# Half of the attention transposes of six head pairs moved from TensorE to VectorE squares and a trip through DRAM

## The chip, the cores and the metric

The kernel runs on one core of a Trainium2 chip: TensorE (PE, its weight loads PEld), VectorE (DVE), ScalarE (ACT), GpSimd (POOL) and SyncE (SP), which only issues transfers. The metric is the time of one execution on the device in microseconds.

## What is computed

One layer with batch 1, 1024 positions and width 1024, in float32. The normalised input is modulated and projected to queries, keys, values and gates of 16 heads of width 64. Eight heads are stick-breaking, eight are forgetting attention. Each is causal, in blocks of 128 queries:

```python
# forgetting head, query block qs:ke
s = q[qs:ke] @ k[:ke].T * scale + (f_q[:, None] - f_k[None, :])
p = softmax(where(k_pos <= q_pos, s, -inf));  out = p @ v[:ke]
# stick-breaking head
z = q[qs:ke] @ k[:ke].T * scale
log_keep = where(k_pos < q_pos, log_sigmoid(-z), 0)
later = cumsum(log_keep, reverse=True) - log_keep
w = where(k_pos < q_pos, exp(log_sigmoid(z) + later), 0);  out = w @ v[:ke]
```

The outputs are gated, go through one output projection, and a residual with a second normalisation ends the layer.

## The kernel before

Heads are worked in pairs p = 0 to 7; pairs 0 to 3 are stick-breaking, 4 to 7 forgetting. Float32 products are made from two rounded parts: an operand is split into a high part (a cast) and a low part (a subtraction), and two or three matmuls are added up. A **unit** (p, h, i) is head h of pair p with query block i; it has i+1 key blocks of 128 columns. Within a head units run with i rising in pairs 0 to 3 and falling in pairs 4 to 6.

The main loop goes over the 128 units with step k. In step k TensorE gets, in this order: the scores of unit k (`att_scores`, L427 and L428), some matmuls of the projections of later pairs (`fill`: lines L270 to L272 for queries, keys and gates, L327 to L329 for values), a product with the values if one is ready (`att_pv`, L493), the transposes of unit k-2 (`att_transpose`, L478; LAG is 2), and more `fill`. A product takes two neighbouring units, so that of the first of the two comes four steps after its scores. TensorE's order is fixed by the program; those of the other engines and of SyncE are made by a scheduler when the program is built, and each runs its queue strictly in order.

In pairs 0 to 3 the scores S go through two sigmoids on ScalarE (L447, L448), a scan on VectorE (L453, L457) and a product with GpSimd (L461). The scan's second operand is a constant kept in PSUM. In pairs 4 to 7 VectorE adds the forget rows `fb` and takes the row's extreme (L434), ScalarE makes the exponential and its sum (L440), VectorE the reciprocal (L441), GpSimd the scaled rows (L442). Then TensorE turns each 128x128 block into PSUM tile T (L478), ScalarE casts T to the high part (L480) and VectorE subtracts for the low part (L481). After the product, ScalarE, VectorE and GpSimd make the gated output `ty` (L512 to L514), and SyncE writes it to DRAM (L522). VectorE adds the causal mask to `fb` ahead of time (L412), from a PSUM copy except the first time.

GpSimd also splits all projection weights (`fetch_w`, L123 to L126; SyncE loads them by L121), and beside pairs 3 to 5 the output projection's, scaled by the gate, which SyncE writes to DRAM (L830, L831) and nobody reads before pair 7.

Tiles that matter: S has one buffer of two banks; T two; the pool `att`, from which `kp`, `be`, `a` and `fb` come, six of 128x1024.

Of the kernel before, what the change touches and what calls it, by code (L numbers as in the profile page):

```python
# [13 lines left out]
P = 128  # L14
# [13 lines left out]
def tile_hybrid_layer(  # L28
# [82 lines left out]
    f_dr = dr.tile([8, SEQ], F32, tag="f_dr", name="f_dr")  # L111

# [132 lines left out]
    def evac_k(p, ch, acc, kst, klo, heads):  # L245
        s = slice(ch * 512, ch * 512 + 512)
        for h in heads:
            r = slice(h * HD, h * HD + HD)
            o = slice((1 - h) * HD, (1 - h) * HD + HD)
            first = nc.scalar.copy(kst[h][r, s], acc[r, :])  # L250
            kf = kst[h].bitcast(F32)
            nc.sync.dma_start(kf[o, s], kf[r, s])
            if p not in CASTS_FIRST:
                last = nc.vector.tensor_tensor(klo[r, s], acc[r, :], kf[r, s], op=ALU.subtract)
        if p in CASTS_FIRST:
            for h in heads:
                r = slice(h * HD, h * HD + HD)
                last = nc.vector.tensor_tensor(klo[r, s], acc[r, :], kst[h].bitcast(F32)[r, s], op=ALU.subtract)  # L258
        return first, last
# [106 lines left out]
    def forget_rows(lf):  # L366
# [17 lines left out]
        nc.sync.dma_start(f_dr.rearrange("h (t p) -> (h t) p", p=P), fr)  # L384
# [22 lines left out]
    def att_causal(u):  # L407
        p, h, i = u
        if p >= 4:
            f = fb[2 * (p - 4) + h]  # L410
            dg = slice(i * P, i * P + P)
            nc.vector.tensor_tensor(f[:, dg], f[:, dg], ps_causal[0][:, :P] if ps_causal else causal, op=ALU.add)  # L412

    def att_scores(u, following):
# [4 lines left out]
        w = ke // ns  # L419
        qs = slice(i * P, i * P + P)  # L420
# [3 lines left out]
        S = s_tile(f"S_{p}_{h}_{i}")  # L424
        for s in range(ns):
            ks = slice(s * w, s * w + w)
            nc.tensor.matmul(S[:, s, :w], qst[p][h][:, qs], kst[p][h][:, ks], start=True, stop=False)  # L427
            nc.tensor.matmul(S[:, s, :w], z, klo[p][:, ks], start=False, stop=True)  # L428
        v3 = lambda a: a[:, :ke].rearrange("p (a b) -> p a b", a=ns)
        if p >= 4:  # L430
# [3 lines left out]
            rows = nc.vector.tensor_tensor_reduce(out=v3(a), in0=S[:, :ns, :w], in1=v3(f),  # L434
# [7 lines left out]
            nc.gpsimd.tensor_scalar(a[:, :ke], a[:, :ke], l, 1.0, op0=ALU.mult, op1=ALU.mult)  # L442
            st_w[u] = a
        else:
# [17 lines left out]
            nc.gpsimd.memset(be[:, ke - 1:ke], 0.0)  # L462
            st_w[u] = be

    def att_transpose(u):
        p, h, i = u
        a = st_w.pop(u)
        j, qo = i // 2, (i % 2) * P
        for g in range((i // 4) + 1):
            n = min(4, i + 1 - 4 * g)  # L470
            if (p, h, j, g) not in st_pt:
                st_pt[p, h, j, g] = [pt_tile(x, f"pt{x}_{p}_{h}_{j}_{g}", F32R, [P, 4, 256])
                                     for x in range(2)]
            hi, lo = st_pt[p, h, j, g]
            tp = t_tile(f"T_{p}_{h}_{i}_{g}")
            for b in range(n):
                kb = 4 * g + b
                nc.tensor.transpose(tp[:, b * P:(b + 1) * P], a[:, kb * P:(kb + 1) * P], ident)  # L478
            t3 = tp[:, :n * P].rearrange("p (a b) -> p a b", a=n)
            nc.scalar.copy(hi[:, :n, qo:qo + P], t3)  # L480
            nc.vector.tensor_tensor(lo[:, :n, qo:qo + P], t3, hi.bitcast(F32)[:, :n, qo:qo + P],  # L481
                                    op=ALU.subtract)
# [521 lines left out]
    for k in range(len(units) + LAG + 1):  # L1004
        if k < len(units):
# [13 lines left out]
            if 4 <= p < NPAIR - 1 and i == 0:  # L1019
                load_fb(2 * (p - 4) + h + 2)  # L1020
# [3 lines left out]
        if LAG <= k < len(units) + LAG:  # L1024
            u = units[k - LAG]
            att_transpose(u)
            seen.add(u)
            if (u[0], u[1], u[2] ^ 1) in seen:
# [76 lines left out]
```

## Time and profile before

| what | value |
|---|---|
| time, median of 3 runs | 685.13 us (685.02 to 685.16) |
| the profiled execution's own time | 685.25 us |
| its span | 683.5 us |
| TensorE clock granted | 0.999 |
| start of the first scores of pair 1, 4, 5, 6, 7 | 137.64, 346.13, 419.02, 489.29, 551.66 us |
| DMA moved | 81.60 MB, 45036 packets |

In the rows of the profile a group reads: line, engine, operation, output<-input by the program's names, shapes, count, then busy time and mean duration in ns, then idle time of the engine just ahead and who ended it. A row of the timeline begins with start and duration in us. A row of DMA issues ends with size and median time from issue to landing. A row of stretches gives for each engine the busy time in that stretch, then clock, DMA share and GB/s. Matmuls overlap, so their durations add up to more than the time that they take.

### The profile page before, as it was taken

Reading aid. Unit: us, or ns where it says so; the run is one execution under the profiler, and the core shown is the slowest. Engines: PE = TensorE matmul, PEld = TensorE weight load, DVE = VectorE, ACT = ScalarE, POOL = GpSimd, SP = SyncE. Lnnn points to the kernel's source line nnn. Section 1 sums busy time; section 2 is a strip of 40 time slices with the busy share of each in tenths; the row PEclk is TensorE's granted clock in tenths of the full one; section 3 lists DMA queues with packets and bytes.
Section 4 is the critical chain, followed back from the end, with each engine's and each line's share of the span. In section 5 each row is a group of like instructions: output and inputs, shape, how many; then the busy total and the mean of one; then the engine's idle time right before and its main releaser. Section 6 shows DMA issues by size and latency. Waiting matters only on the chain.

```text
span 683.5 us, 11770 instructions
## 1 busy us (share of the span) xinstructions
PE 667.2 (98%) x4021; PEld 587.2 (86%) x4021; DVE 450.6 (66%) x914; ACT 382.0 (56%) x861; POOL 427.7 (63%) x558
## 2 busy tenths in 40 slices
PE   5999999999999999999999999999999999999995
PEld 4789898888998888889988888899988889888885
DVE  6785368867666667676675665765566677774645
ACT  5668357856567666566675564655565667531000
POOL 5558977756348566556388896877584364665411
PEclk9999999999999999999999999999999999999999
DMA  9966231112102121122144563453341298143301
GB/s 338 410 236 233 82 105 44 41 29 60 29 9 86 27 57 54 37 55 55 55 131 136 172 176 121 143 166 129 101 150 40 72 327 318 58 162 118 123 31 62
DMA packets 45036, 81.60 MB, mean 119 GB/s; under 512 B 5232, under 2 KB 18864, under 8 KB 44976
## 3 DMA queue, kind: packets, MB, share of 16 engines
q1 hardware_dynamic: 43536, 76.63, 33.8%
q10 hardware_dynamic: 1440, 4.21, 2.2%
q8 instruction: 32, 0.52, 0.3%
q14 instruction: 28, 0.23, 0.1%
HBM read 60.34 MB, written 16.29 MB: 112 GB/s over the span
## 4 chain that ended last, share of the span: by engine, by line
PE 94%; DMA 3%; DVE 2%; ACT 0%; issue 0%; POOL 0%; DVEq 0%
PE m L270 10%; PE m L272 10%; PE m L271 10%; PE pv L493 10%; PE T L478 9%; PE S L428 5%; PE S L427 5%; PE o L884 4%; PE o L882 4%; PE o L883 4%; PE v L327 4%; PE v L328 4%; PE v L329 4%; DMA raws<-in_w_qkg_dram 2%; PE st_late L589 1%; PE st_q L589 1%
## 5 line engine op out<-in xcount | busy, mean ns | idle before, releaser
L270 PE MATMUL m<-uh,whi 128*128 128x512 f32 x304 | 126.4, 416 | 0.0
L272 PE MATMUL m<-uh,wlo 128*128 128x512 f32 x304 | 119.7, 394 | 0.0
L271 PE MATMUL m<-ul,whi 128*128 128x512 f32 x304 | 119.7, 394 | 0.0
L481 DVE TENSOR_TENSOR pt<-T,pt 128x512 fp32r<-128x512 f32 (+2 forms) x192 | 100.5, 550 | 17.5 <-ACT pt L480 16.5
L461 POOL TENSOR_TENSOR be<-be,kp 128x127 f32<-128x127 f32 (+3 forms) x64 | 77.2, 1207 | 33.1 <-DVE kp L457 23.5
L480 ACT CAST pt<-T 128x512 fp32r<-128x512 f32 (+2 forms) x192 | 85.8, 480 | 16.1 <-PE T L478 12.5
L453 DVE TENSOR_TENSOR_SCAN kp<-kp,floor 128x512 f32<-128x512 f32 (+2 forms) x64 | 65.2, 1018 | 31.2 <-ACT kp L447 30.1
L493 PEld LDWEIGHTS pv<-pt,v 128*128 128x128 f32 (+1 forms) x640 | 77.1, 163 | 4.4 <-DVE pt L481 0.7
L493 PE MATMUL pv<-pt,v 128*128 128x256 f32 (+3 forms) x640 | 80.4, 271 | 0.5 <-DVE pt L481 0.5
L442 POOL TENSOR_SCALAR a<-a,l 128x1024 f32<-128x1024 f32 (+3 forms) x64 | 48.1, 751 | 40.3 <-DVE l L441 26.7
L272 PEld LDWEIGHTS m<-uh,wlo 128*128 128x128 f32 x304 | 57.1, 188 | 13.6
L440 ACT ACTIVATE a<-a,nm 128x1024 f32<-128x1024 f32 (+3 forms) x64 | 49.8, 778 | 33.8 <-DVE nm L434 32.7
L427 PE MATMUL S<-k,q 128*128 128x512 f32 (+5 forms) x192 | 66.5, 348 | 0.2 <-DVE nm L434 0.2
L428 PE MATMUL S<-kl,qz 128*128 128x512 f32 (+5 forms) x192 | 65.5, 342 | 0.0
L270 PEld LDWEIGHTS m<-uh,whi 128*128 128x128 f32 x304 | 57.3, 188 | 8.5 <-DVE kl L258 0.2
L271 PEld LDWEIGHTS m<-ul,whi 128*128 128x128 f32 x304 | 57.4, 189 | 8.0
L434 DVE CUSTOM_DVE_ANT_0 a<-S,fb 128x1024 f32<-128x1024 f32 (+3 forms) x64 | 48.3, 755 | 20.1 <-PE S L428 9.3
L514 POOL TENSOR_TENSOR ty<-ty,sg 64x256 f32<-64x256 f32 x64 | 47.5, 742 | 22.3 <-DVE ty L513 11.1
L447 ACT ACTIVATE kp<-S 128x128 f32<-128x128 f32 (+3 forms) x64 | 41.7, 652 | 31.6 <-PE S L428 29.4
L327 PE MATMUL v<-whi_v,uh 128*128 128x256 f32 (+1 forms) x192 | 56.0, 292 | 0.0
L405 ACT CAST qz<-q 64x128 fp32r<-64x128 f32 x128 | 37.4, 295 | 33.2 <-PE S L428 31.8
L328 PE MATMUL v<-whi_v,ul 128*128 128x256 f32 (+1 forms) x192 | 54.2, 282 | 0.0
(285 smaller groups left out, 1593.6 us busy)
## 6 DMA issues: line engine op xcount, KB each, us to landing
raw<-in_w_qkg_dram SPq DMA_DIRECT2D x38, 256.0 KB, 2.9
wss<-in_w_ss_dram SPq DMA_DIRECT2D x16, 512.0 KB, 8.4
x<-in_x_dram SPq DMA_DIRECT2D x8, 512.0 KB, 6.9
k<-k SPq DMA_DIRECT2D x32, 128.0 KB, 2.3
wg<-in_w_gate_dram SPq DMA_DIRECT2D x8, 512.0 KB, 4.9
raw_o<-in_w_out_dram SPq DMA_DIRECT2D x16, 256.0 KB, 2.8
fb<-f_dr ACTq DMA_DIRECT2D x8, 512.0 KB, 4.3
wo_dr<-whi_o SPq DMA_DIRECT2D x16, 256.0 KB, 2.5
```

Source lines behind the costliest of these rows:

```text
L270: nc.tensor.matmul(acc, hi[:, c], u_hi[kt][:, s], start=(kt == 0), stop=False)
L271: nc.tensor.matmul(acc, hi[:, c], u_lo[kt][:, s], start=False, stop=False)
L272: nc.tensor.matmul(acc, lo[:, c], u_hi[kt][:, s], start=False, stop=(kt == NB - 1))
L327: nc.tensor.matmul(acc[:, :n], u_hi[kt][:, ts_], hi[:, s], start=(kt == 0), stop=False)
L328: nc.tensor.matmul(acc[:, :n], u_lo[kt][:, ts_], hi[:, s], start=False, stop=False)
L427: nc.tensor.matmul(S[:, s, :w], qst[p][h][:, qs], kst[p][h][:, ks], start=True, stop=False)
L428: nc.tensor.matmul(S[:, s, :w], z, klo[p][:, ks], start=False, stop=True)
L453: scan = nc.vector.tensor_tensor_scan(rv, rv, floor[0][:, 512 - n:][:, ::-1], initial=0.0, op0=ALU.mult, op1=ALU.max)
L461: nc.gpsimd.tensor_tensor(be[:, :ke - 1], be[:, :ke - 1], kp[:, 1:ke], op=ALU.mult)
L480: nc.scalar.copy(hi[:, :n, qo:qo + P], t3)
L481: nc.vector.tensor_tensor(lo[:, :n, qo:qo + P], t3, hi.bitcast(F32)[:, :n, qo:qo + P], op=ALU.subtract)
L493: nc.tensor.matmul(acc[:m, q0:256], vt[p][:, kb, h * P:h * P + m], pt[:, kb % 4, q0:], start=start, stop=stop)
```

## The change

In pairs 1 to 6 one unit of every two neighbours, the one that comes first in the head's order (i even in pairs 1 to 3, odd in 4 to 6), is no longer turned by TensorE. VectorE transposes each 32x32 square of its rows (into the finished `kp` tile in pairs 1 to 3, into a new `att` tile `sq` in 4 to 6), SyncE writes the result to a DRAM tile `far`, and after that four transfers read it back, one for each 32 target partitions, in runs of (i+1) x 128 bytes. The rows come back turned, in SBUF. ScalarE casts them as it did T; the low part is subtracted by GpSimd in pairs 4 to 6 and for the second group of four key blocks in pairs 1 to 3, by VectorE for the first group there. In pairs 4 to 6 the scaling of a moved unit's rows goes from GpSimd to ScalarE. A moved unit's cast and subtraction are issued together with its neighbour's transposes, one step later than its own transposes were. The forget rows of the next head are loaded one step later. `quartered` is false for every pair, so what depends on it stays as it was; the cut below leaves it out.

```diff
+    def by_blocks(t, n, natural):
+        return t[:, :n * P].rearrange("p (k s c) -> p k s c" if natural else "p (s k c) -> p k s c", k=n, s=4)
+    def on_dma(u):
+        p, h, i = u
+        return i % 2 == (p >= 4) and 0 < p < NPAIR - 1
...
-            nc.gpsimd.tensor_scalar(a[:, :ke], a[:, :ke], l, 1.0, op0=ALU.mult, op1=ALU.mult)
+            if moved:
+                nc.scalar.activation(a[:, :ke], a[:, :ke], AF.Copy, scale=l)
+                squares = att_tile(f"sq_{p}_{h}_{i}")
+                nc.vector.transpose(by_blocks(squares, i + 1, False), by_blocks(a, i + 1, True))
+                through_dram(u, squares, a)
+            else:
+                nc.gpsimd.tensor_scalar(a[:, :ke], a[:, :ke], l, 1.0, op0=ALU.mult, op1=ALU.mult)
...
             nc.gpsimd.memset(be[:, ke - 1:ke], 0.0)
+            if moved:
+                nc.vector.transpose(by_blocks(kp, i + 1, False), by_blocks(be, i + 1, True))
+                through_dram(u, kp, be)
...
+    def through_dram(u, src, dst):
+        p, h, i = u
+        ke, run = (i + 1) * P, (i + 1) * 32
+        far = dr.tile([P, SEQ], F32, tag="far", bufs=4, name=f"far_{p}_{h}_{i}")
+        nc.sync.dma_start(far[:, :ke], src[:, :ke])
+        for s in range(4):
+            nc.sync.dma_start(dst[s * 32:s * 32 + 32, :ke].rearrange("k (q r) -> k q r", q=4),
+                              far[:, s * run:s * run + run].rearrange("(q k) r -> k q r", q=4))
...
+            if on_dma(u):
+                full = a[:, :(i + 1) * P].rearrange("p (q k c) -> p k q c", q=4, c=32)[:, 4 * g:4 * g + n]
+                parts = [t[:, :n, qo:qo + P].rearrange("p k (q c) -> p k q c", q=4)
+                         for t in (hi, hi.bitcast(F32), lo)]
+                nc.scalar.copy(parts[0], full)
+                eng = nc.gpsimd if p >= 4 or g else nc.vector
+                eng.tensor_tensor(parts[2], full, parts[1], op=ALU.subtract)
+                continue
...
-            if 4 <= p < NPAIR - 1 and i == 0:
-                load_fb(2 * (p - 4) + h + 2)
+            if k > 64 and i == NB - 1 and units[k - 1][2] == 0 and 2 * (p - 4) + h + 1 < 8:
+                load_fb(2 * (p - 4) + h + 1)
...
-            att_transpose(u)
+            other = (u[0], u[1], u[2] ^ 1)
+            if not on_dma(u):
+                att_transpose(u)
+                if on_dma(other):
+                    att_transpose(other)
```

On VectorE, in pair 2, head 0, the rows between the scan of unit 6 (`kp_2_0_6`) and that of unit 7 read before:

```order
L457 SCALAR_TENSOR_TENSOR kp_2_0_6_2806<-kp_2_0_6_2806,floor_882 128x384
L513 TENSOR_TENSOR ty_2_0_1_2830<-pv_2_0_1_2821,ty_2_0_1_2830 64x256
L481 TENSOR_TENSOR pt1_2_0_2_0_2836<-T_2_0_4_0_2837,pt0_2_0_2_0_2835 128x4x128
L481 TENSOR_TENSOR pt1_2_0_2_1_2845<-T_2_0_4_1_2846,pt0_2_0_2_1_2844 128x128
L242 SCALAR_TENSOR_TENSOR q_3_0_2686<-m_3_0_1_2781,q_3_0_2686 64x512
L453 SCALAR_TENSOR_TENSOR kp_2_0_7_2865<-kp_2_0_7_2865,floor_882 128x512
```

The same place now (`pt1` is a low part, `T` a turned block in PSUM, `be` the weights of a unit in SBUF):

```order
L513 SCALAR_TENSOR_TENSOR kp_2_0_6_2833<-kp_2_0_6_2833,floor_882 128x384
L550 TENSOR_TENSOR pt1_2_0_2_0_2916<-be_2_0_4_2736,pt0_2_0_2_0_2915 128x4x128
L593 TENSOR_TENSOR ty_2_0_1_2864<-pv_2_0_1_2855,ty_2_0_1_2864 64x256
L255 SCALAR_TENSOR_TENSOR q_3_0_2706<-m_3_0_1_2804,q_3_0_2706 64x512
L520 STREAM_TRANSPOSE kp_2_0_6_2833<-be_2_0_6_2834 128x7x4x32
L509 SCALAR_TENSOR_TENSOR kp_2_0_7_2884<-kp_2_0_7_2884,floor_882 128x512
```

The subtraction of unit 4 takes both inputs from SBUF, and comes first; the squares of unit 6 are new and stand behind it and two others.

On SyncE, from the end of pair 4 into pair 5, the queue read before:

```order
L522 DMA y_dr_91<-ty_4_1_1_5131 64x256
L121 DMA raw_v3_2_5529<-in_w_v_dram 128x512
L121 DMA raw_v3_3_5535<-in_w_v_dram 128x512
L522 DMA y_dr_91<-ty_4_1_0_5224 64x256
L121 DMA raw_o5_1_5570<-in_w_out_dram 128x512
```

The same place now (`far` is the DRAM tile of a moved unit, `wo_dr` the output projection's split weights in DRAM):

```order
L529 DMA far_5_0_7_5163<-sq_5_0_7_5161 128x1024
L602 DMA y_dr_91<-ty_4_1_1_5190 64x256
L910 DMA wo_dr_92<-whi_o4_1_5359 128x512
L911 DMA wo_dr_92<-wlo_o4_1_5360 128x512
L134 DMA raw_v3_0_5572<-in_w_v_dram 128x512
L531 DMA a_5_0_7_5153<-far_5_0_7_5163 32x4x256 x4
L910 DMA wo_dr_92<-whi_o5_0_5502 128x512
L529 DMA far_5_0_5_5263<-sq_5_0_5_5261 128x768
```

Between the write of a unit's squares and its four reads stand an output's write, two writes of split weights and a load.

More of the change, by code (lines that the diff above doesn't have):

```diff
@@ L246, in evac_k, with made, home @@
         s = slice(ch * 512, ch * 512 + 512)
+        def made(t, r):
+            return t[r, :].rearrange("p (k s c) -> p k s c", k=4, s=4) if quartered(p) else t[r, :]
+        def home(t, r):
+            if not quartered(p):
+                return t[r, s]
+            return t[r, :].rearrange("p (s k c) -> p k s c", s=4, c=32)[:, 4 * ch:4 * ch + 4]
         for h in heads:
@@ L383, in forget_rows @@
         nc.scalar.copy(fr, ft)
-        nc.sync.dma_start(f_dr.rearrange("h (t p) -> (h t) p", p=P), fr)
+        if quartered(4):
+            for hh in range(8):
+                nc.sync.dma_start(f_dr[hh].rearrange("(s t c) -> t s c", s=4, c=32),
+                                  fr[8 * hh:8 * hh + 8, :].rearrange("t (s c) -> t s c", s=4))
+        else:
+            nc.sync.dma_start(f_dr.rearrange("h (t p) -> (h t) p", p=P), fr)
         yield
@@ L411, in att_causal @@
             dg = slice(i * P, i * P + P)
[L412 removed]
+            tri = ps_causal[0][:, :P] if ps_causal else causal
+            fd = f[:, dg]
+            if quartered(p):
+                fd = f.rearrange("p (s k c) -> p k s c", s=4, c=32)[:, i]
+                tri = tri.rearrange("p (s c) -> p s c", s=4)
+            nc.vector.tensor_tensor(fd, fd, tri, op=ALU.add)
     def att_scores(u, following):
@@ L419, in att_scores @@
         w = ke // ns
+        moved = on_dma(u)
+        quarters = quartered(p)
+        run = (i + 1) * 32
         qs = slice(i * P, i * P + P)
```

38 lines of the change are left out of this document (29 added, 9 removed).

## The prediction

> **What bounds the kernel now.** I read the page first (which engine is full, at which clock), then the chain that ended last by line, then the busy time of each engine by stage, with the stages cut where the first scores of pairs 1, 4, 5, 6 and 7 start, then groups by shape for the prices.
>
> ```profile
> span 683.5 us, 11770 instructions
> PE 667.2 (98%) x4021; PEld 587.2 (86%) x4021; DVE 450.6 (66%) x914; ACT 382.0 (56%) x861; POOL 427.7 (63%) x558
> ...
> by line: PE m L270 10.3%; PE m L272 10.2%; PE m L271 10.2%; PE pv L493 10.0%; PE T L478 9.1%; PE S L428 4.9%; PE S L427 4.9%; PE o L884 4.4%; PE o L882 4.4%; PE o L883 4.4%; PE v L327 4.2%; PE v L328 4.1%; PE v L329 4.1%; DMA raws<-in_w_qkg
> ```
>
> ```profile
> core 0: us, PE busy (x) PEld busy (x) DVE busy (x) ACT busy (x) POOL busy (x), PEclk, DMA share, GB/s
> 137.64:346.13 208.49, 208.49 (x1363) 189.28 (x1361) 142.17 (x237) 134.66 (x303) 120.78 (x167) 1.00 0.17 48
> 346.13:419.02 72.89, 72.89 (x423) 63.42 (x422) 45.22 (x114) 41.09 (x98) 62.66 (x69) 1.00 0.50 155
> 419.02:489.29 70.27, 70.27 (x491) 65.13 (x490) 44.08 (x119) 39.78 (x104) 50.94 (x58) 1.00 0.38 120
> 489.29:551.66 62.37, 62.11 (x360) 53.30 (x358) 41.76 (x109) 38.50 (x93) 35.86 (x44) 1.00 0.38 110
> ```
>
> The first window holds pairs 1 to 3, the others pairs 4, 5 and 6: all that the change touches. TensorE is busy in 413.76 of these 414.02 us, at clock 1.00, and the chain runs almost wholly over its lines. So in this stretch whatever leaves TensorE shortens the kernel, as long as nothing else makes TensorE wait. The second thing to see is GpSimd in pair 4: 62.66 of 72.89 us, far above VectorE and ScalarE.
>
> **What leaves TensorE.** In pairs 1 to 3 the moved units are i = 0, 2, 4, 6 with 1+3+5+7 = 16 of a head's 36 blocks, in pairs 4 to 6 i = 1, 3, 5, 7 with 20. Six heads each: 96 + 120 = 216 of the 576 transposes. The price of one is not its busy time, since matmuls overlap, but its share of the chain: 9.1% of 683.5 us over 576 is 0.108 us. The timeline agrees:
>
> ```profile
> 241.62 0.39 PE L272 MATMUL m<-uh,wlo 128*128 128x512 f32 x1
> 241.85 0.82 PE L478 MATMUL T<-ident,be 128*128 128x128 f32 x6
> 242.43 0.48 PE L270 MATMUL m<-uh,whi 128*128 128x512 f32 x1
> 242.74 0.39 PE L271 MATMUL m<-ul,whi 128*128 128x512 f32 x1
> ```
>
> From 241.85 to 242.74 stand six transposes and one product; a product takes 0.23 (241.62 to 241.85), which leaves 0.66, or 0.11 each. 216 x 0.108 = 23.3 us: 10.4 in pairs 1 to 3, 8.6 in 4 and 5, 4.3 in 6. No matmul is added or made longer. [...]
>
> **What is added to engines beside TensorE.** The prices:
>
> ```profile
> L481 DVE TENSOR_TENSOR pt<-T,pt 128x512 fp32r<-128x512 f32 x96 | 64.6, 686 | 16.8 <-ACT pt L480 16.3
> L481 DVE TENSOR_TENSOR pt<-T,pt 128x128 fp32r<-128x128 f32 x32 | 9.0, 281 | 0.1
> L480 ACT CAST pt<-T 128x512 fp32r<-128x512 f32 x96 | 54.8, 587 | 7.7 <-PE T L478 5.0
> L447 ACT ACTIVATE kp<-S 128x1024 f32<-128x1024 f32 x8 | 8.2, 1028 | 3.5 <-PE S L428 3.5
> L442 POOL TENSOR_SCALAR a<-a,l 128x1024 f32<-128x1024 f32 x8 | 9.0, 1130 | 5.1 <-DVE l L441 5.1
> L442 POOL TENSOR_SCALAR a<-a,l 128x256 f32<-128x256 f32 x8 | 3.9, 487 | 6.1 <-DVE l L441 3.2 <-PE v L329 2.8
> L126 POOL TENSOR_TENSOR wlo<-raw,whi 128x512 fp32r<-128x512 f32 x38 | 49.1, 1297 | 2.4 <-DMA wo_dr<-wlo_o 0.8
> L453 DVE TENSOR_TENSOR_SCAN kp<-kp,floor 128x512 f32<-128x512 f32 x40 | 48.8, 1219 | 24.3 <-ACT kp L447 23.7 <-issue 0.2
> ```
>
> The trace shows no transpose by squares. From below it is the subtraction's slope, (686 - 281)/384 = 1.05 ns a column, so 1.2 us for 1024; from above the scan's 1219/512 = 2.4 ns, so 2.4 us. I take 1.2, since one pass over one input is the nearer kind. VectorE then gets 16 x 128 columns, about 2.7 us, in a head of pairs 1 to 3, and hands 0.8 us of subtractions to GpSimd; in pairs 4 to 6 it gets 3.3 and hands over 3.5. ScalarE scales rows instead of GpSimd (at most 1.03 us for 1024 columns); its casts only change their source. At 68% and 65% in pairs 1 to 3 and less later, both have room: nothing on the sum.
>
> GpSimd has not. In pairs 4 to 6 it loses four scalings a head, between 1.13 and 0.49, 3.2 us, and gains the subtraction of 2560 columns at 1.297/512, 6.5 us: plus 3.3 a head, 6.6 a pair. Pair 4: 62.7 + 6.6 = 69.3 us of work in 72.9 - 4.3 = 68.6; pair 5: 57.5 in 66.0. It just fits if the output projection's splits, which nobody awaits here, run a little earlier; it leaves no slack.
>
> **The new path, and who waits at its end.** A product of two units comes four units after the first one's scores, before and after. Two heads show the room:
>
> ```profile
> 235.18 0.37 PE L428 MATMUL S<-kl,qz 128*128 128x448 f32 x1
> ...
> 254.62 1.64 PE L493 MATMUL pv<-pt,v 128*128 128x256 f32 x13
> ...
> 384.93 0.39 PE L428 MATMUL S<-kl,qz 128*128 128x512 f32 x1
> ...
> 403.44 1.73 PE L493 MATMUL pv<-pt,v 128*128 128x256 f32 x14
> ```
>
> In pair 2 the last score of unit 6 ends at 235.55 and its product starts at 254.62: 19.1 us, less 12 blocks no longer turned in between, 17.8. In pair 4, unit 7: 385.32 to 403.44, 18.1 less 10 blocks, 17.0. What must fit there:
>
> ```profile
> L434 DVE CUSTOM_DVE_ANT_0 a<-S,fb 128x1024 f32<-128x1024 f32 x8 | 9.7, 1216 | 2.1 <-PE S L428 2.1
> L440 ACT ACTIVATE a<-a,nm 128x1024 f32<-128x1024 f32 x8 | 9.2, 1152 | 6.4 <-DVE nm L434 6.4
> L440 ACT ACTIVATION_READ_ACCUMULATOR a<-a,nm 128x1 f32 x64 | 12.0, 187 | 0.0
> L441 DVE RECIPROCAL l<-l 128x1 f32<-128x1 f32 x64 | 10.4, 162 | 25.6 <-ACT a L440 24.4 <-POOL wlo L126 0.3 <-POOL whi_o L125 0.3
> L448 ACT ACTIVATE be<-S 128x896 f32<-128x896 f32 x8 | 7.3, 912 | 0.0
> L461 POOL TENSOR_TENSOR be<-be,kp 128x895 f32<-128x895 f32 x8 | 14.2, 1774 | 4.2 <-DVE kp L457 4.2
> ```
>
> ```profile
> k<-k SPq DMA_DIRECT2D x32, 128.0 KB, 2.3
> ...
> xr<-in_x_dram SPq DMA_DIRECT2D x8, 512.0 KB, 3.4
> wol<-wo_dr SPq DMA_DIRECT2D x8, 512.0 KB, 7.7
> ...
> yr<-y_dr SPq DMA_DIRECT2D x8, 256.0 KB, 3.4
> ```
>
> ```profile
> L522 SPq DMA_DIRECT2D y_dr<-ty x56: 445/452/811, 103.8 to 564.1; - x56
> L412 DVE TENSOR_TENSOR fb<-fb,ps_causal x63: 269/286/290, 350.1 to 604.7; 128x128 f32<-128x128 f32 x63
> ...
> L412 DVE TENSOR_TENSOR fb<-fb,causal x1: 1106/1106/1106, 346.5 to 346.5; 128x128 f32<-128x128 f32 x1
> ```
>
> The trip through DRAM is unknown. Its write moves up to 512 KB (3.4 by xr). Its four reads move at most 128 KB each in short runs: 2.3 by k at best, 3.4 by yr, which also reads short runs; I take 2.5, since yr moves twice as much. They are issued 0.45 apart, so the last lands 3 x 0.45 + 2.5 = 3.9 us after the first issue, itself held until the write has landed. From above stands wol's 7.7, where several large loads share the queue.
>
> Unit 7 of pairs 4 to 6: 1.22 + 1.15 + 0.19 + 0.16 + scaling 1.03 + squares 1.2 = 5.0; write 3.4; reads 3.9; cast 0.6; two subtractions on GpSimd 2.6: 15.5 of 17.0 us. Every step stands in an in-order queue behind other work, on engines 56 to 95% full; a fifth to a third of a microsecond at each of nine steps is 1.8 to 3 us, so the product waits 0.3 to 1.5. The cast also stands ahead of other work on ScalarE: when it waits for a landing, the next exponentials wait with it. I take 1.4 us a head.
>
> Unit 6 of pairs 1 to 3: two sigmoids 1.8 beside the scan, which ends at 0.9 + 7 x 128 columns at 2.4 ns = 3.1; product on GpSimd 1.8; squares 1.0; write 3.2; reads 3.9; two casts 1.1; last subtraction 1.0: 15.1 of 17.8 us. But the squares now stand on VectorE behind the subtraction of unit 4, which waits for its own landing, and that subtraction reads two SBUF tiles. What this can cost shows in L412: one addition with its mask in SBUF took 1.106 us, 63 with the mask in PSUM 0.286, so up to 0.8 us a time beside a busy GpSimd. [...] With 0.7 for the subtraction itself, 0.8 for the lock and 1.1 for two instructions passed, 2.6 of the 2.7 us of slack are gone before any queueing; I take 1.0 us a head.
>
> Sum against the profiled execution, 685.25 us (span 683.5 and 1.75 around it; the median of the runs, 685.13, is 0.12 less): 685.25 - 23.3 + 6 x 1.0 + 6 x 1.4 = 676.3, rounded to 676.
>
> **The rivals.**
> - *All hidden.* The waits of a head fall into each other's shadow and TensorE stays full: 685.25 - 23.3 = 662. For it: 1.5 and 2.7 us of slack without queueing, and all engines but GpSimd below 70%. Against it: nine queues in a row. Chance 0.20.
> - *GpSimd takes over in pairs 4 and 5 only.* TensorE gains 10.4 + 4.3 where GpSimd has room, and nothing of the 8.6 where it is full: 670.5. For it: 69.3 of 68.6 us in pair 4. Against it: the splits can run ahead. Chance 0.11.
> - *The trip is too long: slower.* SyncE's one queue gets five issues per moved unit, four of them behind a landing, and weight loads, gate outputs and the projection's writes stand in the same queue between write and reads, so a landing of 2.5 becomes 4 or 5, on the way to wol's 7.7. Two microseconds more per trip make 3.0 and 3.4 us a head: 685.25 - 23.3 + 6 x 6.4 = 700. It decides from 23.3/12 = 1.94 us of waiting a head, 0.7 above what I take. For it: GpSimd's lateness holds SyncE too, because some of these transfers wait for it. Chance 0.25.
> - The forecast keeps 0.44; its own range is 668 to 683, waits of 0.5 to 1.8 us a head.
>
> **How the numbers follow.** A measurement here tells 0.2%, 1.4 us, from no change. Faster: 0.40 of the forecast's 0.44, all of the first two rivals, 0.71. Same: 0.03 of the forecast and 0.02 of the slow rival, 0.05. Slower: 0.24. The range must reach from the hidden case to the lighter half of the slow one: 660 to 694, outside of which about 0.03 and 0.14 lie. The doubled price of squares (plus 1.2 us a head, 14 in all) and the shorter reads lie within it.
>
> **What would show it.** Right: 360 transposes left on TensorE; its idle time 10 to 20 us more than before, in front of pv and S in pairs 1 to 6, released by VectorE, ScalarE or GpSimd; ScalarE's casts of moved units waiting for DMA; the four reads landing near 2.5 us. Wrong: TensorE as full as before in these pairs (hidden), its idle in pairs 4 and 5 alone with GpSimd over 95% (second rival), over 23 us idle with reads landing at 4 us or later (third), or a square costing twice what I took.

## The result and the profile after

| what | before | after |
|---|---|---|
| time, median of 4 runs | 685.14 us (685.02 to 685.18) | 722.21 us (721.17 to 724.87) |
| ratio of the two | | 1.0547, 95% interval 1.0517 to 1.0577 |
| profiled execution, span | 685.25, 683.5 us | 724.87, 723.2 us |
| TensorE clock granted | 0.999 | 0.971 |

The kernel became 5.5% slower, where 1.3% faster was forecast, and the time lies outside the range. The profiled run is the longest of the four after. The page of the kernel after, its first lines and the chain that ended last:

```profile
span 723.2 us, 11984 instructions
PE 664.9 (92%) x3805; PEld 574.9 (79%) x3805; DVE 463.5 (64%) x914; ACT 398.1 (55%) x885; POOL 456.4 (63%) x582
...
PE 54%; DMA 16%; DVE 7%; POOL 6%; ACT 6%; issue 6%; SPq 3%; ACTq 0%; POOLq 0%; DVEq 0%
```

216 matmuls have gone (x4021 to x3805), as they should, but TensorE's share fell to 92%, and the chain leaves it for almost half of its length. DMA, which the change put in, now has 16% of it. Busy times by stage, cut as before where the first scores of pairs 1, 4, 5, 6 and 7 start; the last row runs to the end:

```profile
core 0: us, PE busy (x) PEld busy (x) DVE busy (x) ACT busy (x) POOL busy (x), PEclk, DMA share, GB/s
139.10:358.20 219.10, 204.51 (x1274) 181.84 (x1272) 159.52 (x252) 134.75 (x306) 131.20 (x180) 0.98 0.37 104
358.20:437.80 79.60, 72.89 (x376) 61.27 (x376) 43.11 (x108) 46.40 (x103) 65.91 (x70) 0.95 0.61 192
437.80:513.90 76.10, 68.93 (x450) 61.94 (x448) 42.63 (x114) 45.09 (x111) 57.89 (x62) 0.98 0.60 189
513.90:583.10 69.20, 61.75 (x320) 50.92 (x318) 40.04 (x104) 43.62 (x102) 42.30 (x49) 0.95 0.57 172
583.10:723.20 140.10, 127.43 (x657) 107.68 (x657) 83.03 (x178) 39.37 (x97) 60.40 (x82) 0.96 0.41 143
```

The same last stretch of the kernel before, which the prediction did not need:

```profile
551.66:683.50 131.84, 124.99 (x660) 105.92 (x658) 82.33 (x176) 38.89 (x95) 58.54 (x80) 0.99 0.41 149
```

Before, TensorE was full in the first four stretches. Now it is idle for 219.1 - 204.5 = 14.6 us in pairs 1 to 3, and for 6.7, 7.2 and 7.5 us in pairs 4, 5 and 6; in the last stretch its idle time grew from 6.9 to 12.7 us. The second thing to see is the clock: 1.00 in pairs 1 to 6 before, 0.95 to 0.98 now. It also makes the busy column misleading: at half clock the same matmuls are busy for longer (a 128x512 product of the scores took 0.63 us at 358.76, and 0.39 at 346.44 in the kernel before).

What TensorE waited for, and the longest waits of ScalarE and VectorE:

```profile
engine line waited for: us in total, times, longest us
PE S L474 <- DVE nm L484: 14.7, 9, 3.7
PE pv L573 <- ACT pt L548: 7.4, 2, 4.4
PE pv L573 <- DVE pt L561: 5.9, 5, 2.3
PE S L474 <- ACT be L504: 5.0, 2, 4.2
...
ACT pt L548 <- DMA a<-far: 40.0, 20, 4.9
ACT pt L548 <- DMA be<-far: 35.1, 19, 3.7
...
DVE a L484 <- DMA far<-sq: 14.5, 9, 3.5
```

Only 7.4 us are products that wait for a cast of rows from DRAM. The largest part, 19.7 us, is scores that wait for their one PSUM buffer, because VectorE or ScalarE has not read the scores before. ScalarE in turn stands 75.1 us in front of casts whose rows have not landed, with everything queued behind them (not all of that is lost: e17 below has 72.7 us of it and takes 20 us less). And VectorE stands 14.5 us in front of its first instruction on new scores (L484), because the `att` tile for its result is still being written to DRAM as `sq`.

**One place, read through.** ScalarE at the end of pair 3, from its timeline:

```profile
354.37 0.62 ACT L548 CAST pt<-be 128x512 fp32r<-128x512 f32 x1 [3.46 <-DMA be<-far]
...
355.73 1.03 ACT L503 ACTIVATE kp<-S 128x1024 f32<-128x1024 f32 x1
...
357.06 1.06 ACT L504 ACTIVATE be<-S 128x1024 f32<-128x1024 f32 x1
```

TensorE at the same place, from its timeline, and the stretches around it:

```profile
358.17 0.79 PE L474 MATMUL S<-k,q 128*128 128x512 f32 x1 [4.15 <-ACT be L504]
358.76 0.63 PE L475 MATMUL S<-kl,qz 128*128 128x512 f32 x1
359.19 0.63 PE L474 MATMUL S<-k,q 128*128 128x512 f32 x1
```

```profile
350.00:354.00 4.00, 4.00 (x33) 3.70 (x31) 1.63 (x3) 0.56 (x2) 3.83 (x5) 1.00 0.81 259
354.00:358.00 4.00, 0.02 (x1) 0.00 (x0) 2.98 (x4) 3.63 (x8) 2.54 (x4) 0.78 0.83 267
358.00:362.00 4.00, 3.83 (x9) 3.06 (x10) 3.64 (x8) 2.23 (x5) 3.12 (x4) 0.50 0.61 174
362.00:366.00 4.00, 4.00 (x23) 3.51 (x23) 1.28 (x5) 2.96 (x5) 4.00 (x4) 0.87 0.26 99
```

The cast waits 3.46 us for its rows. The two sigmoids of the newest scores stand behind it and run late; they are the readers of S, so the next scores start 4.15 us late. No product waits here at all. Then comes a second price: the clock falls to half, and products of 128x512 that stood 0.23 us apart (241.62 to 241.85 in the kernel before) now stand 0.43 apart (358.76 to 359.19). The shortfall of these four rows, (0.22 + 0.50 + 0.13) x 4 = 3.4 us, is two steps of 1.7, each half a clock for 3.4 us. Taken over 2 us windows from 90 to 690 us, the kernel after has ten such steps in six places, 17.1 us in all, the kernel before none ahead of 680.

The profiled executions differ by 39.7 us of span, and 23.3 us of matmul left TensorE, so 63.0 us were lost. Of these 36.0 are TensorE's idle time in pairs 1 to 6 and 5.8 what it grew by behind them; pair 1 starts 1.5 later, behind a half-clock stretch at 14.9 us that the profiled run of the kernel before does not have (no unit is moved ahead of pair 1, and e5, which moves none, has such a stretch at 14.2); the clock is up to 17.1, less the part that falls into waits. That makes 60.4 at most, and some 3 us are left unassigned.

### The profile page after: what moved, and what is told of

Its sections match the earlier page's. It is cut to its first block, busy times and chain, and to the rows that moved or that the text cites. A ratio compares the mean times of both kernels' runs of the same rounds, so it can differ in the third digit from the quotient of the medians.

```text
span 723.2 us, 11984 instructions
## 1 busy us (share of the span) xinstructions
PE 664.9 (92%) x3805; PEld 574.9 (79%) x3805; DVE 463.5 (64%) x914; ACT 398.1 (55%) x885; POOL 456.4 (63%) x582
## 2 busy tenths in 40 slices
DMA packets 79598, 109.92 MB, mean 152 GB/s; under 512 B 18288, under 2 KB 49584, under 8 KB 79536
## 4 chain that ended last, share of the span: by engine, by line
PE 54%; DMA 16%; DVE 7%; POOL 6%; ACT 6%; issue 6%; SPq 3%; ACTq 0%; POOLq 0%; DVEq 0%
PE pv L573 6%; PE m L297 5%; PE m L298 4%; PE m L299 4%; PE o L964 4%; PE o L962 4%; PE o L963 4%; PE T L558 3%; DMA be<-far 3%; DMA a<-far 3%; SPq L531 2%; DMA far<-sq 2%; PE S L474 2%; PE S L475 2%; PE v L354 2%
## 5 line engine op out<-in xcount | busy, mean ns | idle before, releaser
L299 PE MATMUL m<-uh,wlo 128*128 128x512 f32 x304 | 121.8, 401 | 0.0
L298 PE MATMUL m<-ul,whi 128*128 128x512 f32 x304 | 121.7, 400 | 0.0
L573 PE MATMUL pv<-pt,v 128*128 128x256 f32 (+3 forms) x640 | 87.4, 280 | 18.2 <-ACT pt L548 7.4
L573 PEld LDWEIGHTS pv<-pt,v 128*128 128x128 f32 (+1 forms) x640 | 80.7, 170 | 26.6 <-ACT pt L548 8.3
L474 PE MATMUL S<-k,q 128*128 128x512 f32 (+5 forms) x192 | 68.0, 355 | 19.8 <-DVE nm L484 14.7
L484 DVE CUSTOM_DVE_ANT_0 a<-S,fb 128x1024 f32<-128x1024 f32 (+3 forms) x64 | 48.1, 752 | 34.1 <-DMA far<-sq 14.5
L560 ACT CAST pt<-T 128x512 fp32r<-128x512 f32 (+3 forms) x120 | 55.9, 479 | 24.3 <-PE T L558 22.7
L561 DVE TENSOR_TENSOR pt<-T,pt 128x512 fp32r<-128x512 f32 (+3 forms) x120 | 63.5, 548 | 7.8 <-ACT pt L560 7.0
L474 PEld LDWEIGHTS S<-k,q 128*128 128x128 f32 x192 | 36.7, 191 | 29.2 <-DVE nm L484 18.5
L356 PE MATMUL v<-wlo_v,uh 128*128 128x256 f32 (+1 forms) x192 | 54.9, 286 | 0.0
L550 POOL TENSOR_TENSOR pt<-a,pt 128x512 fp32r<-128x512 f32 (+1 forms) x36 | 39.6, 1102 | 24.1 <-ACT pt L548 23.5
```

Of the source, the lines that this page charges most:

```text
L298: nc.tensor.matmul(acc, hi[:, c], u_lo[kt][:, s], start=False, stop=False)
L299: nc.tensor.matmul(acc, lo[:, c], u_hi[kt][:, s], start=False, stop=(kt == NB - 1))
L474: nc.tensor.matmul(sp, qst[p][h][:, qs], kh, start=True, stop=False)
L573: nc.tensor.matmul(acc[:m, q0:256], vt[p][:, kb, h * P:h * P + m], pt[:, kb % 4, q0:], start=start, stop=stop)
```

## The experiments

Theory when they began: the rows land too late, and ScalarE's casts pass the delay on. First rival: the added work of VectorE, GpSimd and ScalarE is late by itself. Second rival, from the waits above: the trip holds too many `att` tiles. The table has the length in us of three parts of the program, from the starts of the first scores of pairs 1, 4 and 7 and the span of each profiled run. "Less its matmuls" is the kernel before without the moved transposes.

| run | time, ratio to before | pairs 1-3 | pairs 4-6 | pair 7 to the end |
|---|---|---|---|---|
| before | 685.1 | 208.5 | 205.5 | 131.8 |
| less its matmuls (worked out) | 662 | 198.1 | 192.6 | 131.8 |
| after | 722.2, 1.055 | 219.1 | 224.9 | 140.1 |
| e1, no trip | 682.3, 0.996 | 210.9 | 200.3 | 131.9 |
| e9, trip unused | 709.8, 1.037 | 211.3 | 228.4 | 131.9 |
| e15, trip unused, one row tile | 701.6, 1.023 | 208.6 | 223.7 | 131.6 |
| e10, no squares | 709.3, 1.035 | 210.7 | 221.9 | 137.8 |
| e11, cast one step later | 725.1, 1.057 | 221.2 | 229.1 | 134.6 |
| e13, one row tile | 715.2, 1.044 | 213.8 | 223.3 | 136.9 |
| e17, one row tile, and the cast one step later in pairs 4 to 6 | 701.7, 1.024 | 214.6 | 216.2 | 132.2 |

**No trip.** ScalarE and the subtractions read the squares directly; the output's rows are then in the wrong order.

```diff
-                through_dram(u, squares, a)
+                a = squares
...
-                through_dram(u, kp, be)
+                be = kp
```

> The squares stay, the trip through DRAM goes: the casts and subtractions of a moved unit read the tile of squares where it lies (so the 32x32 squares are not put in their places, and the output is not the reference's). Same instructions on TensorE, VectorE, ScalarE and GpSimd as in the changed kernel; 240 transfers fewer. Theory A (the trip: ScalarE's casts stand in order and wait for landings, 75 us in the trace, and what stands behind them makes TensorE wait): 660 to 668 us, TensorE without idle in pairs 1 to 6. Theory B (the work added to VectorE and GpSimd, and the lock between them, is what makes TensorE wait): stays above 690 us. Without waits the clock should be back at 1.00.

682.31 us, ratio 0.9957 (0.994 to 0.9973). The trip is worth 40 us, but 20 us of loss stay without it: the time lies between the two expectations. TensorE's waits in this run:

```profile
PE pv L573 <- POOL pt L550: 4.8, 4, 2.7
PE pv L573 <- DVE pt L561: 3.2, 3, 1.9
PE pv L573 <- POOL be L518: 3.0, 2, 2.2
```

With four smaller ones these are 14.9 us, and three clock steps ahead of 660 us make at most 5.1: 20.0 of the 20.4 us by which its span of 680.6 stands above 683.5 - 23.3. So the first rival holds for a third of the loss. Of the 14.9 us of waits, 7.8 end with GpSimd, 5.4 with VectorE and 1.7 with ScalarE. Pair 3 alone is 9.7 us longer than its 68.8 us before less 32 transposes; these are its second head's last steps:

```profile
297.00:313.00 16.00, 12.38 (x73) 10.54 (x72) 15.04 (x19) 9.41 (x19) 10.16 (x11) 0.95 0.22 59
```

VectorE, the third engine in the row, is busy for 15.04 of 16 us there, though over the pair it is below 80% (58.3 of 75.0). That its full queue there is what makes the products late is read from this row, not shown by a run of its own.

**Pairs 1 to 3 and pairs 4 to 6 alone.** `on_dma` with `0 < p < 4`, and with `4 <= p < NPAIR - 1`.

> Only pairs 1 to 3 take the new path. In the changed kernel their stretch took 10.6 us more than before, pairs 4 to 6 19.4 and pair 7 8.3. If the stretches are independent: 692 to 697 us. If pairs 1 to 3 only suffered from what pairs 4 to 6 do to the queues: 675 to 680, the forecast's gain.

> Only pairs 4 to 6 take the new path. If the stretches are independent, and pair 7's loss comes from pair 6: 685 + 19 + 8 = 712 us (706 to 716). If the loss in pairs 4 to 6 was carried over from pair 3: under 695.

694.79 (1.0139, 1.0124 to 1.0155) and 706.69 us (1.032, 1.0297 to 1.0342): both parts lose, 9.7 and 21.6 us, together 31.3 of the 37.1. No single pair spoils the whole.

**What a wait costs.** The kernel before, with pauses of known length in TensorE's order.

```diff
+    def pause(n, trip, name):
+        for d in range(n + 1):
+            t = t_tile(f"pz_{name}_{d}")
+            nc.tensor.transpose(t[:2, :P], px, ident)
+            if d < n and trip:
+                nc.scalar.copy(py[:2, :], t[:2, :2])
+                nc.scalar.dma_start(px[:2, :], py[:2, :])
+            elif d < n:
+                nc.scalar.copy(px[:2, :], t[:2, :2])
```

> The kernel before, all transposes on TensorE, with 12 pauses put into TensorE's order ahead of the scores of unit 3 of every head of pairs 1 to 6: a small transpose that waits for a copy of the transpose before it. Pairs 1 and 4: two round trips over ScalarE (short, about 1 us each pause); pairs 2 and 5: one round trip over ScalarE and a small DMA (about 2.5 to 3 us); pairs 3 and 6: two such round trips in a row (5 to 6 us). If a pause costs only its own length: 685 plus the sum of the 12 pauses, about 4 x (1 + 3 + 5.5) = 38, so 723. If a long pause also lowers the granted clock for some microseconds, as in the changed kernel: 3 to 4 us more for each of the 4 or 8 long ones, 735 to 755, with windows behind the long pauses at clock 0.5 and those behind the short ones at 1.0.

740.88 us (1.0816, 1.079 to 1.0842), inside the range for pauses that also lower the clock. The waits of TensorE, and the stretches from two pauses of a single small DMA on, one of 2.23 us ending at 269.01 and one of 2.33 us ending at 517.91:

```profile
PE pz L997 <- DMA bss_sb<-bss_sb: 27.7, 12, 3.5
PE pz L997 <- DVE pt L481: 4.9, 3, 1.8
PE pz L997 <- ACT bss_sb L1002: 2.4, 8, 0.6
```

```profile
266.80:270.21 3.41, 1.20 (x7) 1.04 (x8) 1.38 (x2) 1.53 (x4) 1.87 (x3) 1.00 0.33 69
270.21:273.62 3.41, 3.41 (x12) 2.86 (x11) 1.63 (x2) 1.56 (x5) 1.19 (x2) 0.50 0.28 105
...
515.97:519.38 3.41, 1.47 (x11) 1.41 (x12) 0.60 (x1) 0.30 (x1) 0.49 (x2) 1.00 0.22 79
519.38:522.79 3.41, 3.41 (x32) 3.41 (x32) 1.54 (x7) 2.05 (x6) 1.86 (x2) 1.00 0.00 0
```

The span grew by 59.0 us for 35.0 us of waiting. After the first pause the clock is at half for 3.41 us, a shortfall of 1.71 us, and TensorE is busy all through it, so it is paid in full. Twelve such steps, 20.5 us, follow the pauses of this run; the other 3.5 us were not told apart (32 small transposes were added, and pair 1 starts 1.0 us later). The pauses of at most 0.6 us in pair 1 brought none. Of the six places with 2.1 to 3.7 us of waiting in all, five brought one step and one, the pause of 2.33 us, none; of the four with two small DMAs in a row, 4.1 to 5.5 us, three brought two steps and one brought one.

What tells the two pauses above apart is where they lie. Within a run all half-clock stretches lie on one grid of 3.41 us: in the kernel after they begin at 318.70, 356.24, 421.10, 458.64, 537.15 and 595.18 us, which is 11, 19, 11, 23 and 17 times 3.41 us apart. The first pause falls into one cell of it whole, the second is cut by a grid line at 515.97, so that only 1.94 us of it lie in one cell. Over the 20 profiled executions, from 60 us on to 30 us before the end, all 58 cells at full clock in which TensorE was idle for 2.0 us or more were followed by a cell at half clock (six of them in the kernel after, with 2.2 to 3.0 us of idle time), none of the 3347 with less than 1.4 us, and 13 of the 44 between.

**A trip that nobody uses.** TensorE turns every block as before; squares, write and reads are made all the same, and read back into the squares' own tile. In e6 GpSimd scales the rows as it did before, in e9 ScalarE does, as in the changed kernel.

```diff
-                through_dram(u, squares, a)
+                through_dram(u, squares, squares)
...
-            if on_dma(u):
+            if False:
```

> The changed kernel with TensorE still turning every block, so that nothing waits for the rows from DRAM; squares, write and four reads are made as before the change was undone, but read back into the tile of the squares and used by nobody. Theory that the wait for the landing is what costs: 685 to 692, close to the kernel before, since only att buffers and VectorE's 1.2 us squares are added. Rival that the load costs (SyncE's queue blocked by waiting reads and writes, six att buffers, the squares on VectorE): over 700 although nobody uses the rows.

713.65 us (1.0409, 1.0393 to 1.0425): the theory that only the wait for landings costs fell here.

> The run with the unused trip again, but with the scaling of moved rows on ScalarE, as in the changed kernel: in the run with the unused trip it stood on GpSimd, and VectorE's squares waited 21.7 us for it, so that pairs 4 to 6 were 9.5, 5.7 and 11.4 us longer than before while pairs 1 to 3 stayed within 2.6. If those 26 us came from the squares waiting for GpSimd: 685 to 692 now, and what the changed kernel loses in pairs 4 to 6 is the wait for landings. If they came from SyncE's queue (late weights) and the att buffers, which the trip loads used or not: 700 or more.

709.83 us (1.0369, 1.0304 to 1.0435): squares waiting for GpSimd were not the reason either. Of the loss 22.9 us lie in pairs 4 to 6 and 2.6 in pair 3, at whose end the first forget rows are loaded; VectorE's waits name the tiles:

```profile
DVE a L484 <- DMA sq<-far: 13.6, 5, 6.9
```

**Tiles.** First the forget rows loaded five steps later, then one tile of them for all heads. The latter leaves out seven loads and uses the first head's rows for all.

```diff
     def load_fb(hh):
+        if hh:
+            fb[hh] = fb[0]
+            return
         fb[hh] = att_tile(f"fb_{hh}")
```

> As the changed kernel, but the forget rows of the next head are loaded five units later, so that for most of a head one of the six att buffers is free for the tiles of the new path. Theory C (in pairs 4 to 6 the wait is for a buffer: VectorE's first step stood 14.5 us for the write of squares to land, and TensorE 14.7 us for VectorE's first step): most of these 14.7 us and of the clock lost behind them go: 695 to 708 us. Theory A (landings in front of ScalarE's casts): within 4 us of the changed kernel's 722.

716.89 us (1.0459, 1.042 to 1.0498), 5.3 less than the kernel after, between the two expectations.

> The changed kernel with one tile of forget rows: those of the first forgetting head are loaded once and used for all eight (the other seven loads are left out), which gives pairs 4 to 6 one att tile more for most of the time. If the scarce tiles are what the changed kernel loses in pairs 4 to 6 (19.3 us there over before): 10 to 15 us back, 707 to 712. If the wait for landings is: 717 or more, since the trip keeps its length.

> The control: the kernel before with the same single tile of forget rows. TensorE is full in pairs 4 to 6 and nothing waits for a tile there, so 685 within 1 us; anything faster has to be taken off the gain of the runs with one tile.

> The run with the unused trip and ScalarE's scaling (709.8) with one tile of forget rows. If that run's 25 us were tiles held for the trip: 688 to 696. If they were SyncE's queue or VectorE's squares: 704 or more.

> The run with squares and casts but without the trip (682.3) with one tile of forget rows. It shows what the engines' own work leaves of the 23.3 us when neither landings nor tiles count: if tiles mattered even without the trip, 675 to 679; if the engines' order and GpSimd are what is left, 680 to 683.

e13 715.17 us (1.0442, 1.0423 to 1.0461), e14 686.06 (1.0013, 1.0004 to 1.0022), e15 701.63 (1.0225, 1.0201 to 1.025), e16 683.61 (0.9967, 0.995 to 0.9985). e13 and e15 fell between what their two theories expected; e16 shows that without the trip the tile gains nothing (682.31 us in e1). VectorE's wait for a tile that is still written to DRAM, 14.5 us in the kernel after, is down to 0.4 in e13, and yet pairs 4 to 6 gained only 1.6 us of their 19.3; pairs 1 to 3, whose end meets the first loads of forget rows, gained 5.3. ScalarE's wait for rows stays:

```profile
ACT pt L551 <- DMA a<-far: 42.0, 21, 5.0
...
ACT pt L551 <- DMA be<-far: 32.0, 17, 3.5
```

e15 shows the two halves apart. Its stretches are pairs 1 to 3 and pairs 4 to 6:

```profile
137.50:346.10 208.60, 208.60 (x1362) 189.30 (x1361) 158.00 (x261) 134.55 (x303) 120.72 (x167) 1.00 0.36 102
346.10:569.80 223.70, 210.96 (x1268) 185.26 (x1267) 147.71 (x365) 136.35 (x317) 129.44 (x145) 0.98 0.58 180
```

In pairs 1 to 3 all squares, writes and reads run, and TensorE is full at clock 1.00 in 208.60 us, where the kernel before takes 208.49: there squares and trip as a load cost a full TensorE nothing. (Whether they would beside a TensorE with 10.4 us less to do, this run does not show.) In pairs 4 to 6 the same load costs 18 us though nobody waits for its rows. VectorE still waits for tiles there (16.3 us in five waits for `sq`, which is held for the whole trip in this run).

**Other engines.** All low parts of moved units on VectorE, without the trip (`eng = nc.vector`); and the trip without the squares (`through_dram(u, a, a)` and `through_dram(u, be, be)`).

> The squares without the trip (rows in the wrong order, as in the run without the trip: 682.3) and with all low parts of moved units on VectorE, none on GpSimd. If the 20 us that the run without the trip stands above TensorE's own 662 come from GpSimd's lateness: 666 to 675, with GpSimd's 6.5 us a head gone. If they come from VectorE (the lock on two inputs in SBUF, its order): 682 or more, since it gets 6.5 us more a head.

690.18 us (1.0064, 1.0036 to 1.0092): VectorE has no room for them; GpSimd is late with its share in e1, and still the better place for it. Whether e1's own loss is GpSimd's or VectorE's this run does not tell, since it loads one where it frees the other.

> The changed kernel with the trip but without the squares (rows come back in the wrong order): 2.7 to 3.3 us a head less on VectorE, one step less in the chain, and in pairs 4 to 6 no att tile for the squares. If landings and the scarce att buffers cost most: in pairs 1 to 3, where the number of tiles stays, 1 us a step shorter chain gives at most 5 us back; in pairs 4 to 6, where a tile goes, 10 to 15: 703 to 710. If VectorE's extra work is no part of it and buffers are not either: 715 to 722.

709.32 us (1.0349, 1.0311 to 1.0387), 13 less. In pairs 1 to 3, where no tile is saved, the 5 us expected became 8.4, and what is left there (210.7) is what e1 has without any trip (210.9). So taking away either gives back the same 8 us there, and the 12.7 us that stand above 198.1 remain both times; a run without either was not made.

**More time to land.** The casts of a moved unit and its product one step later, first everywhere, then in pairs 4 to 6 with the one row tile.

```diff
+        for u in late:
+            att_transpose(u)
+            ready.append((u[0], u[1], u[2] // 2))
+        late.clear()
```

> The changed kernel with the casts of a moved unit and its product one step later, so that the rows have a step more (3 to 6 us) to land. If the window of 17 to 18 us was too short: 700 to 710, with the casts' 75 us of waiting for DMA mostly gone. If the tiles are then held too long (six att buffers) or the work of the other engines ends last: 718 or more.

725.08 us (1.0566, 1.052 to 1.0613). No product waits for a cast any more, but scores wait for VectorE and ScalarE, 34.6 us instead of 19.7, and VectorE still 8.4 for tiles:

```profile
PE S L474 <- DVE nm L484: 21.1, 12, 4.7
PE S L474 <- ACT be L504: 13.5, 8, 5.7
```

> The run with one tile of forget rows (715.2), and in pairs 4 to 6 the casts of a moved unit and its product one step later as well. Alone, each of the two gave little there (a tile: 17.7 instead of 19.3 us over before; a step: 20.4 or more, with TensorE's waits moved from the products to the scores that wait for tiles). If landings and tiles are one loss that changes its place (whichever is relieved, the other ends last), both together give 10 us or more back: 705 or less. If VectorE's and ScalarE's order is the rest: 712 or more.

701.67 us (1.024, 1.022 to 1.0261). Alone the later cast lost 3 us and the tile gained 7; the two together, the cast in pairs 4 to 6 only, gain 20.5. In pairs 4 to 6 alone the later cast lost 4.2 us, the tile gained 1.6, and the two together gain 8.7. That is what the expectation for one loss in two places said: relieve one wait, and the other ends last.

**Keeping a part.** Without units 6 and 7; pair 1 alone; pair 1 without its last large unit.

> Only units below 6 take the new path: i = 0, 2, 4 in pairs 1 to 3, 1, 3, 5 in pairs 4 to 6; 9 and 12 blocks a head instead of 16 and 20, 126 transposes, worth 13.6 us. If the long chain of the largest units is what is late: 674 to 682, each pair 1 to 3 us shorter than before. If the trip costs by its number of transfers, tiles and queue places: 695 to 710, three quarters of the changed kernel's loss.

> Only pair 1 takes the new path. Pair 1 was 2.1 us shorter in the changed kernel and every later pair longer: 682.5 to 683.5 if that holds alone (0.2 to 0.4% faster than before), 685 or more if what pair 1 gains is given back in pair 2, whose projections are then no further ahead.

> Only pair 1 takes the new path, and of it not the last large unit (head 1, unit 6), whose lateness the run with pair 1 alone showed in the first steps of pair 2 (1.5 us of its 2.4 given back): 25 transposes, 2.7 us less work on TensorE. 682.3 to 683 if pair 2 then stays at 67.5 us, 684.6 if it does not.

e12: 705.46 us (1.0297, 1.0275 to 1.032), so the long chains are not the only ones that are late. e8: 684.61 (0.9994, 0.9985 to 1.0003): pair 1 is 2.4 us shorter and pair 2 1.5 longer. e18: 685.52 (1.0003, 0.9994 to 1.0012), no difference, though its profiled run had a span of 682.3. No version found here is measurably faster than the kernel before with the same output.

## Why the prediction was wrong

- **What leaves TensorE: right.** e1's pair 1, in which TensorE is full as before, has 25 transposes fewer and is 2.8 us shorter, 0.11 each. The groups show 360 transposes left:

```profile
L558 PE MATMUL T<-ident,be 128*128 128x128 f32 x192 | 27.5, 272 | 1.0 <-DVE pt L561 0.8
L558 PE MATMUL T<-ident,a 128*128 128x128 f32 x168 | 25.8, 280 | 0.0
```

- **Prices of the new operations: right in the middle, without their spread.** Squares were put at 1.2 us for 1024 columns, the largest write at 3.4, the reads at 2.5. The squares took 1.25 in the mean, the largest write and reads 3.5 and 3.1 in the median, but a single read took up to 7.0 us (last row, the reads of pairs 4 to 6):

```profile
L495 DVE STREAM_TRANSPOSE sq<-a 128x1024 f32<-128x1024 f32 x6 | 7.5, 1246 | 4.4 <-ACT a L493 3.7 <-DMA wo_dr<-wlo_o 0.7
```

```profile
far<-sq SPq DMA_DIRECT2D x6, 512.0 KB, 3.5
a<-far SPq DMA_DIRECT2D x24, 128.0 KB, 3.1
...
be<-far SPq DMA_DIRECT2D x24, 16.0 KB, 1.8
```

```profile
DMA to landing us min/median/max: 1.7/2.3/7.0
```

- **"Both have room: nothing on the sum": this step failed.** It was said of VectorE and ScalarE by their busy shares of 65 to 68%. e1 has none of the trip and still lost 20 us: the work comes in bursts, most of all with the largest units at the end of pair 3, and a share over a pair does not show them. GpSimd, of which the prediction said that it just fits, had no term either, and 7.8 of e1's 14.9 us of waits end with it. What the prediction and two expectations call the lock was put at 0.8 us from L412, whose 1.106 us from 346.49 on lie beside GpSimd's split of 346.13 to 347.45 (L126). That one engine locks the other out is shown by no run. A longer time beside GpSimd was seen again, and by more than 0.8 us: the same subtraction on VectorE took 2.09 us at 311.62, with GpSimd's split at 311.87 beside it, and 0.69 at 322.53, where GpSimd was idle:

```profile
311.62 2.09 DVE L550 TENSOR_TENSOR pt<-be,pt 128x512 fp32r<-128x512 f32 x1 [1.67 <-ACT pt L548]
...
322.53 0.69 DVE L550 TENSOR_TENSOR pt<-be,pt 128x512 fp32r<-128x512 f32 x1 [2.83 <-ACT pt L548]
```

- **Waits of 1.0 and 1.4 us a head: this term failed, too small.** TensorE's idle time is 14.6 us over six heads in pairs 1 to 3 and 21.4 in pairs 4 to 6: 2.4 and 3.6 a head, plus 5.8 behind them. The rule was there ("when it waits for a landing, the next exponentials wait with it"), but the sum priced only the product at the chain's end. In the trace ScalarE stands 75.1 us at those casts, and scores wait longer than products do. The chain itself was over its room of 17.8 and 17.0 us too. Means of the six largest units of each kind, from the end of the last score, beside what the sum had:

| part of the chain | unit 6, pairs 1 to 3: put, measured | unit 7, pairs 4 to 6: put, measured |
|---|---|---|
| last score to the end of the squares | 5.9, 8.4 us | 5.0, 6.6 us |
| end of the squares to the first cast (write and reads) | 7.1, 7.4 us | 7.3, 10.1 us |
| first cast to the last subtraction | 2.1, 5.6 us | 3.2, 5.0 us |
| whole | 15.1, 21.4 us | 15.5, 21.8 us |

  The third row holds two casts and two subtractions, in queues with other work between them.
- **No term for tiles.** `sq` takes one more of the six `att` tiles in pairs 4 to 6 until its write has landed, and no step of the prediction counted which tiles are alive at once. e17 against e13 and e11 shows that it counts together with the landing, not beside it.
- **No term for the clock.** Up to 17.1 us, more than the whole waiting that was forecast. e5 shows that it comes from the waits (12 steps, 20.5 us, behind its pauses, and none ahead of 680 us in the kernel before).
- **The rivals.** The slower case was on the list with 0.25 and 700 us, and its sign came true; its mechanism did in part, and only in pairs 4 to 6. In pairs 1 to 3, which lost too, the trip of the largest units took 7.4 us where write and reads had been put at 7.1, and SyncE did not hold it: from the end of the squares to the issue of the write passed 0.16 us (mean of the 24 units). In pairs 4 to 6 the trip of unit 7 took 10.1 us where 7.3 had been put, the two microseconds and more that this rival named: the write was issued 0.6 us behind the squares (0.44 in the mean of all 24 units, 1.3 to 2.4 in four of them), and reads landed late. That is 2.8 of the 6.3 us by which this chain is over its sum. One trip, unit (4, 0, 7), on VectorE, SyncE and ScalarE:

```profile
365.98 1.25 DVE L495 STREAM_TRANSPOSE sq<-a 128x1024 f32<-128x1024 f32 x1 [0.82 <-ACT a L493]
```

```profile
367.25 0.32 SPq L529 DMA_DIRECT2D far<-sq  x1
...
370.67 1.74 SPq L531 DMA_DIRECT2D a<-far  x4
```

```profile
375.85 0.62 ACT L548 CAST pt<-a 128x512 fp32r<-128x512 f32 x1 [2.40 <-DMA a<-far]
```

The write is issued 0.02 us behind the squares, the reads follow 3.4 us later, and the cast runs 8.6 us behind the squares. In pairs 1 to 3 what came late is what stood ahead and behind: from the first scores of unit 6 to its squares passed 8.3 us in the mean of six, of which the scores themselves are some 1.0; the sum had 4.9 for the rest. GpSimd in pair 4 is busy for 65.9 of 79.6 us, no bound, and TensorE is idle in every stage, so the second rival fell, and with it the case that all is hidden; without the trip (e1) GpSimd is busy for 67.4 of pair 4's 72.8 us.

**What stays open.** e17 is 16.5 us above the kernel before, and ScalarE still waits 72.7 us for rows in it; how much of this is landings and how much the bursts of e1 was not told apart. The runs with one row tile also leave out seven loads of 512 KB, so a part of e13's 7 us may be their traffic; e14 only shows that the loads cost the kernel before nothing. A trip issued from another queue than SyncE's was not tried.

## What to carry to other kernels

Work taken off a full engine pays only if no replacement of it stands in an in-order queue ahead of something the full engine waits for (here ScalarE stood 75.1 us at casts, and the readers of the scores stood behind them): list for every new wait what is queued behind it, and who reads that. A wait of a full TensorE cost more than its length here, up to 1.3 times in e1 ((14.9 + 5.1) / 14.9) and 1.6 in e5 ((35.0 + 20.5) / 35.0), because the clock fell to half for 3.41 us behind every cell of its grid with 2.0 us or more of idle time. A step that gets longer also holds its buffers longer; where latency and buffers are both at their limit, relieving one alone can show little (here +2.9 and -7.0 us, together -20.5), and only an experiment on both tells.

## What the runs showed of the hardware

- The granted clock fell in steps of equal size: (1 - clock) summed over a place gave 1.7 or 3.4 us in every place ahead of 660 us of the kernel after, e1, e2, e3, e5 and e17. They lie on a grid of 3.41 us within each run; in the 20 profiled executions a cell with 2.0 us or more of idle TensorE was followed by one at half clock in 58 of 58 cases, one with less than 1.4 us in none of 3347. In a cell already at half clock 0.75 us of idle time were enough for another in 23 of 23 cases, and with less than 0.25 us none of 62 was followed by another.
- The 48 trips raised the bytes moved from 81.60 to 109.92 MB, and the packets from 45036 to 79598. In pairs 1 to 3 of e15 that load, at a DMA share of 0.36, left TensorE's time as it was (208.60 us, 208.49 in the kernel before).
- A VectorE subtraction of 128x512 with both inputs in SBUF took 1.4 us longer beside GpSimd's split (2.09 against 0.69 us), more than the 0.8 that the kernel before showed (L412, 1.106 against 0.286 us). Of the twelve of this size in the kernel after, the five beside which GpSimd did nothing longer than a memset of 0.1 us took 0.69 us each, the seven others 0.80 to 2.35.
